# Giving a split tile's raw buffer to the next transfer as soon as its rest is told, in the v stage of a decoder trunk

## The chip, the cores and the metric

The kernel runs on one core of one Trainium2 chip. The metric is device microseconds of one execution, as a median over several runs. The core has TensorE (PE, with its weight loads shown apart as PEld), VectorE (DVE), ScalarE (ACT), GpSimd (POOL) and SyncE (SP). Work crosses between them by semaphores, and transfers from HBM are issued from the instruction streams of SP, ACT and POOL. Each of these streams is worked off in order: a transfer that has to wait for something holds up what stands behind it in the same stream.

## The reference, cut to what matters

Two pre-norm residual layers run over 256 positions with 1024 channels. The first mixes by attention and retention, the second by a gated short convolution; each is followed by a PEER mixer, which is where the change lies:

```python
def peer(xn, w_q, sub_keys, u, v):
    ...
    def step(args):
        tc, ec, gc = args
        hid = jax.nn.gelu(jnp.einsum('td,thkd->thk', tc, u[ec]), approximate=False)
        return jnp.einsum('thk,thkd->td', gc * hid, v[ec])
```

For each token 8 heads choose 16 of 16,384 experts. An expert has a row of u (1024 numbers) and a row of v (1024 numbers). The output is the sum of the chosen rows of v, weighted by gate times gelu of the token's product with the row of u. All of it is in f32.

## The kernel before

Of the 256 tokens, 96 are done sparsely: their 16,384-row tables are read by indirect transfers from POOL (L1020), 128 rows of 4 KB at a time, 96 such gathers from u and 96 from v in each layer. The other 160 tokens are done densely: the whole of u is multiplied with them, the hidden values are multiplied with a gate matrix that is zero where an expert was not chosen, and the result `HG` is multiplied with the whole of v. So a layer's PEER has a **u stage** and a **v stage** after the scores. The sparse gathers run beside both, one gather at a time being consumed by DVE (L1030 for u, L1041 for v, into `gacc`).

In the v stage v passes as 128 tiles of 128 experts by 1024 channels (512 KB each), in order, one tile a step. Most tiles are **split tiles** (the list `SPL`): ACT casts the raw tile to fp32r (`vhi`, `weight_parts`, L1419), DVE subtracts the cast from the raw tile and writes what is left as bf16 (`vlo`, `weight_rest`, L1426; below this is called telling the rest), and PE multiplies `vhi` with two parts of the hidden values (L1546) and `vlo` with a bf16 copy of them (L1548). After `vlo` is written nobody reads the raw tile again. Tiles 0, 2, 12, 22 and so on to 122, and the last three, are **whole tiles**: PE multiplies the raw tile itself (L1506). The hidden values of two or three neighbouring split tiles are split together by two casts on ACT (L1488, L1489) and one subtraction on DVE (`row_rest`, L1496).

What a step emits is written out by hand. At step i, `carry(i)` emits the `row_rest` of the group before, the casts of hidden values for a group that begins at tile i+3, the cast `vhi` of tile i+3, and the rest `vlo` of tile i+2. Then `st.next()` may issue loads and hands out tile i, PE's products of tile i are emitted, and `ga.step()` may let DVE consume one gather and POOL issue the next. `vhi` and `vlo` each rotate over three buffers.

The raw tiles lie in a ring of 8 buffers (`RAW`), filled by class `Stream`. Tile i uses buffer i mod 8, and loads are issued strictly in tile order (`self.nl` is the next one). In the v stage the loads of even tiles stand in SP's stream, those of odd tiles in ACT's (L151, `src[2]`). Whether the next load may be issued is decided when the program is written out, by `room()`, which asks `free()` of the tile that held the buffer before:

```python
        return i < 0 or (i < self.nu - self.held if self.whole(i) else i < self.ns)
```

A v tile is "whole" for this class (its entry in `srcs` has None), split or not, so it counts as free once it has been handed out and the next `st.next()` comes: at step i the newest load is that of tile i+7. This decides where in the stream the load stands. Beside it, the load carries semaphore waits for the instructions that really read the buffer before: `vlo` of the tile eight before it where that is a split tile, PE's products where it is whole.

Towards the end of the u stage (`i in (NK - QUIET, NK - QUIET + 2)`) `weight_parts` is called for v tiles 1 and 3 with their rests, so `weight_rest` also runs there.

Of the kernel before, what the change touches and what calls it, by code (L numbers as in the profile page):

```python
# [120 lines left out]
class Stream:  # L121
# [6 lines left out]
    def __init__(self, ctx, tc, srcs):  # L128
        self.nc = tc.nc
        self.srcs = srcs  # L130
        pool = ctx.enter_context(tc.tile_pool(name="wraw", bufs=1))
        self.ring = pool.tile([P, RAW, D], F32, tag="raw", name="raw")
        self.hi_pool = ctx.enter_context(tc.tile_pool(name="whi", bufs=3))
        self.lo_pool = ctx.enter_context(tc.tile_pool(name="wlo", bufs=3))
        self.more = None
        self.end = 0
        self.raw = {}
        self.part = {}
        self.nl = 0
        self.held = 0  # L140
        self.ns = 0
        self.nu = 0

# [43 lines left out]

    def free(self, i):

        return i < 0 or (i < self.nu - self.held if self.whole(i) else i < self.ns)  # L190

    def ahead(self, extra=0):
        n = len(self.srcs)
# [30 lines left out]
def trunk_kernel(ctx, tc, x, small, cst, mcst, ew_in, ew_out, ow_in, ow_out, wq, keys, pu, pe_, pv, pun, gains, out):  # L224
# [42 lines left out]
    st = Stream(ctx, tc, srcs)  # L267
# [12 lines left out]
    def nm(s):  # L280
        uid[0] += 1
        return f"{s}{uid[0]}"
# [770 lines left out]
    def peer(l, before, norm):  # L1053
        with tc.tile_pool(name=nm("hg"), bufs=1) as hp:
# [360 lines left out]
            def weight_parts(j, low=True):  # L1415

                raw = st.raw[first + j]
                whi[j] = st.hi_pool.tile([P, D], F32R, tag="hi", name=nm("vhi"))
                act.copy(whi[j], raw)  # L1419
                if low:  # L1420
                    weight_rest(j)

            def weight_rest(j):
                raw = st.raw[first + j]
                wlo[j] = st.lo_pool.tile([P, D], BF16, tag="lo", name=nm("vlo"))
                v.tensor_tensor(wlo[j], raw, whi[j].bitcast(F32), OP.subtract)  # L1426

            first = st.nu + NK - len(PRE)
            for i in range(NK):
# [82 lines left out]
            def carry(i):  # L1512
                j = i + AHEAD
                if "rest" in hsb:
                    row_rest()
                if 4 <= j and j in SPL:
                    if j in RUNS:
                        row_parts(j)
                    weight_parts(j, False)
                if 4 <= j - 1 and j - 1 in SPL:  # L1520
                    weight_rest(j - 1)
# [61 lines left out]
    with tc.manual_schedule():  # L1583
        norms = [Norm(0)]
        nc.sync.dma_start(G, small)
        nc.sync.dma_start(C[:, :P], cst[:, :P])
        for th in range(2):
            (nc.scalar if th else nc.sync).dma_start(h[:, th, :], x[th])
        nc.sync.dma_start(C[:, P:], cst[:, P:])
        v.memset(Z, 0.0)  # L1590
        act.activation(norms[0].w[:, 0, 6:7], Z[:, 0:1], AF.Sqrt)
        for _ in range(3):
            st._load()
        busy(24)
        norms[0].first(hid_tile(nm("junk")))
        a = Norm(1)
        even_mixer(norms[0], a)
        b = Folded(2)
        peer(0, a, b)
        a = Norm(3)  # L1600
        odd_mixer(b, a)
        peer(1, a, Final())
# [40 lines left out]
```

## Time and profile before

| what | value |
|---|---|
| median of 3 runs | 1489.08 us (1485.73 to 1489.53) |
| the profiled execution, as timed | 1486.53 us |
| its span, first to last instruction | 1484.7 us |
| granted TensorE clock, mean | 0.996 |
| HBM read | 527.93 MB |
| v stage of layer 0, products of tile 1 to the last tiles | about 494 us to 752 us |
| v stage of layer 1, the same | about 1215 us to 1475 us |

The span leaves out 1.8 us of the profiled execution's time. The clock is full nearly everywhere, so no stage is slow for that. The rows that matter are the chain that ended last, the wait table of the v stage, the tables of busy time and bandwidth by stretch, and the transfers' queues.

### The profile page before, as it was taken

The numbers are of one execution on the slowest core, as the hardware profiler recorded it, in microseconds if no ns is written. First come the engines' busy times: TensorE is split into PE (matmuls) and PEld (weight loads), VectorE is DVE, ScalarE is ACT, GpSimd is POOL, SyncE is SP. The second block draws the span as 40 slices with busy tenths as digits, with TensorE's granted clock in tenths as the row PEclk, the third lists the DMA queues.
The fourth block names the chain that finished last, engine by engine and source line by source line (L and its number), as shares of the span: only waits on it lengthen the run. The fifth ranks groups of instructions, "written<-read, shape, count | busy, mean of one in ns | idle before, by whom it ended". The sixth has DMA issues, their size and how long they took to land.

```text
span 1484.7 us, 30109 instructions
## 1 busy us (share of the span) xinstructions
PE 1434.1 (97%) x11260; PEld 1327.8 (89%) x11260; DVE 1242.5 (84%) x2505; ACT 804.1 (54%) x1872; POOL 731.1 (49%) x508
## 2 busy tenths in 40 slices
PE   9999999999998999899999999999999999999997
PEld 5667999999998999898898699999999999988887
DVE  5637999968898789999976589997888868999997
ACT  6556412158775555555663463213887745655554
POOL 6754545546664344443244374555655624653540
PEclk9999999999999999999999999999999999999999
DMA  8547899999999999999975589999999999999994
GB/s 323 198 146 253 324 369 393 397 413 412 411 412 407 385 398 405 402 407 408 384 264 180 179 307 346 388 402 404 411 413 410 402 392 396 389 407 406 405 408 172
DMA packets 132164, 531.81 MB, mean 358 GB/s; under 512 B 15217, under 2 KB 15473, under 8 KB 118705
## 3 DMA queue, kind: packets, MB, share of 16 engines
q1 hardware_dynamic: 57024, 257.95, 45.0%
q0 software_dynamic: 56416, 204.29, 34.8%
q10 hardware_dynamic: 18576, 67.64, 11.6%
q8 instruction: 89, 1.46, 0.4%
q14 instruction: 59, 0.48, 0.1%
HBM read 527.93 MB, written 1.05 MB: 356 GB/s over the span
## 4 chain that ended last, share of the span: by engine, by line
DMA 37%; PE 29%; DVE 24%; issue 5%; ACT 2%; POOL 1%; ACTq 0%; SPq 0%; DVEq 0%; POOLq 0%
DMA raw<-pv 25%; DMA rows<-pun,ig 7%; PE hid L1408 7%; DVE rows L1030 4%; PE vo L1546 4%; DMA grow<-pv,ig 3%; PE hid L291 2%; PE vo L1506 2%; DVE hg L1140 2%; DVE grow L1030 2%; DVE hg L1146 2%; DVE hg L1142 2%; PE vo L1548 2%; PE ea L325 2%; DMA rows<-pv,ig 2%
## 5 line engine op out<-in xcount | busy, mean ns | idle before, releaser
L1408 PE MATMUL hid<-xf,raw 128*128 128x160 f32 x3328 | 478.2, 301 | 8.8 <-DVE hg L1449 8.5
L1408 PEld LDWEIGHTS hid<-xf,raw 128*128 128x128 f32 x3328 | 458.2, 191 | 11.7 <-DVE hg L1449 11.6
L1419 ACT CAST vhi<-raw 128x1024 fp32r<-128x1024 f32 x222 | 227.4, 1047 | 205.7 <-DMA raw<-pv 143.1
L1546 PE MATMUL vo<-ko,vhi 128*128 128x320 f32 x1776 | 315.2, 319 | 14.8 <-DVE ko L1496 9.6
L1426 DVE TENSOR_TENSOR vlo<-raw,vhi 128x1024 bf16<-128x1024 f32 x222 | 268.0, 1223 | 47.6 <-ACT vhi L1419 43.2
L1020 POOL DMA_INDIRECT rows<-pv,ig x128 | 199.8, 1561 | 216.4 <-DVE gacc L1041 172.0
L1546 PEld LDWEIGHTS vo<-ko,vhi 128*128 128x128 f32 x1776 | 262.0, 188 | 21.3 <-ACT vhi L1419 14.2
L1020 POOL DMA_INDIRECT rows<-pun,ig x128 | 161.3, 1260 | 118.6 <-DVE rows L1030 61.6
L176 POOL TENSOR_TENSOR lo<-raw,hi 128x1024 bf16<-128x1024 f32 x70 | 167.2, 2397 | 87.0 <-ACT hi L174 80.3
L1030 DVE SCALAR_TENSOR_TENSOR rows<-rows,xg 128x1024 f32<-128x1024 f32 x128 | 155.4, 1220 | 23.6 <-DMA rows<-pun,ig 23.1
L1548 PE MATMUL vo<-hb,vlo 128*128 128x160 bf16 x1776 | 161.4, 234 | 7.1 <-DVE vlo L1426 6.8
L1446 ACT ACTIVATE hg<-hid 128x160 f32<-128x160 f32 (+14 forms) x240 | 62.2, 265 | 194.1 <-PE hid L1408 193.9
L1041 DVE SCALAR_TENSOR_TENSOR gacc<-rows,ghid,gacc 128x1024 f32<-128x1024 f32 x124 | 158.8, 1281 | 6.5 <-DMA rows<-pv,ig 6.2
L1020 POOL DMA_INDIRECT grow<-pv,ig x64 | 91.8, 1434 | 117.9 <-DVE gacc L1041 103.1
L1548 PEld LDWEIGHTS <-vlo 128*128 128x128 bf16 x1776 | 117.4, 98 | 34.1 <-DVE vlo L1426 14.3
L1358 ACT ACTIVATE ko<-ko,idxT 128x128 f16<-128x128 f16 x320 | 101.6, 391 | 38.2 <-DVE ko L1343 38.1
L1020 POOL DMA_INDIRECT grow<-pun,ig x64 | 82.8, 1293 | 78.9 <-DVE grow L1030 50.2
L174 ACT CAST hi<-raw 128x1024 fp32r<-128x1024 f32 x100 | 102.4, 1046 | 30.2 <-issue 19.9
L291 PE MATMUL hid<-x,hi 128*128 128x256 f32 x800 | 108.9, 289 | 3.9 <-DVE z L973 2.0
L291 PEld LDWEIGHTS hid<-x,hi 128*128 128x128 f32 x800 | 100.0, 193 | 4.8 <-issue 2.9
L1361 ACT ACTIVATE ko<-ko,idxT 128x128 f16<-128x128 f16 x320 | 101.2, 389 | 0.0
L1506 PE MATMUL vo<-hg,raw 128*128 128x160 f32 x544 | 83.1, 302 | 1.1 <-DVE hg L1449 1.1
(254 smaller groups left out, 2075.6 us busy)
## 6 DMA issues: line engine op xcount, KB each, us to landing
raw<-pu SPq DMA_DIRECT2D x104, 1024.0 KB, 8.3
raw<-pv SPq DMA_DIRECT2D x128, 512.0 KB, 8.5
raw<-pv ACTq DMA_DIRECT2D x128, 512.0 KB, 7.9
raw<-wq SPq DMA_DIRECT2D x32, 512.0 KB, 4.2
raw<-ew_in SPq DMA_DIRECT2D x28, 512.0 KB, 4.4
raw<-ow_in SPq DMA_DIRECT2D x24, 512.0 KB, 4.9
hg<-pe_ SPq DMA_DIRECT2D x22, 512.0 KB, 6.9
raw<-ew_out SPq DMA_DIRECT2D x8, 512.0 KB, 3.3
```

The source lines that it names most:

```text
L174: self.nc.scalar.copy(hi, t)
L176: eng.tensor_tensor(lo, t, hi.bitcast(F32), OP.subtract)
L291: pe.matmul(ps[:, :S], hi[:, k * P:(k + 1) * P], A2[:, k, s_, :], start=k == 0 and s_ == 0, stop=False)
L1020: gp.indirect_dma_start(self.row(s_), None, table, bass.IndirectOffsetOnAxis(IG[:, 0, s_ % STEPS:s_ % STEPS + 1].bitcast(U32), 0))
L1030: v.scalar_tensor_tensor(r, r, 1.0, XG[:, q % 2, :], op0=OP.mult, op1=OP.mult, accum_out=w)
L1041: v.scalar_tensor_tensor(self.acc[q], r, w, self.acc[q], op0=OP.mult, op1=OP.add)
L1408: pe.matmul(ps[:, :TD], w[k], XF[:, k, :], start=k == 0, stop=k == ND - 1)
L1419: act.copy(whi[j], raw)
L1426: v.tensor_tensor(wlo[j], raw, whi[j].bitcast(F32), OP.subtract)
L1506: pe.matmul(vo[b][:, TG:S], w[:, c], HG[:, i, :], stop=i == NK - 1, **m)
L1546: pe.matmul(vo[b][:, TG:S + TD], hi[:, b * P:(b + 1) * P], hs, **m)
L1548: pe.matmul(vo[b][:, TG:S], lo[:, b * P:(b + 1) * P], hb, **m)
```

## The change

`Stream` gets a set of dead tiles. `free()` says yes for a tile in it. `weight_rest` puts its tile there as soon as the subtraction that reads the raw tile last has been emitted, and asks at once for loads:

```diff
         self.held = 0
+        self.dead = set()
         self.ns = 0
...
     def free(self, i):
 
-        return i < 0 or (i < self.nu - self.held if self.whole(i) else i < self.ns)
+        return i < 0 or i in self.dead or (i < self.nu - self.held if self.whole(i) else i < self.ns)
...
                 v.tensor_tensor(wlo[j], raw, whi[j].bitcast(F32), OP.subtract)
+                st.dead.add(first + j)
+                st.loads()
```

`loads()` was there before; it issues loads as long as `room()` says yes. Loads still go in tile order, so a whole tile that has not been multiplied yet keeps back all that come after it.

## The prediction

> **What bounds the kernel now.** I read the page first: the slices of the span, then the chain that ended last.
>
> ```profile
> span 1484.7 us, 30109 instructions
> ...
> PE   9999999999998999899999999999999999999997
> ...
> GB/s 323 198 146 253 324 369 393 397 413 412 411 412 407 385 398 405 402 407 408 384 264 180 179 307 346 388 402 404 411 413 410 402 392 396 389 407 406 405 408 172
> ...
> DMA 37%; PE 29%; DVE 24%; issue 5%; ACT 2%; POOL 1%; ACTq 0%; SPq 0%; DVEq 0%; POOLq 0%
> DMA raw<-pv 25%; DMA rows<-pun,ig 7%; PE hid L1408 7%; DVE rows L1030 4%; PE vo L1546 4%; DMA grow<-pv,ig 3%; PE hid L291 2%; PE vo L1506 2%; DVE hg L1140 2%; DVE grow L1030 2%; DVE hg L1146 2%; DVE hg L1142 2%; PE vo L1548 2%; PE ea L325 2%; DMA rows<-pv,ig 2%
> ```
>
> PE is shown busy nearly all the time, yet the largest single piece of the chain, a quarter of the span, is the transfer of raw v tiles. A slice is 37.1 us, so the v stages are slices 14 to 20 and 33 to 40. The highest bandwidth in any slice is 413 GB/s. Next I read the two v stages by stretches: engines' busy time, granted clock, DMA share, GB/s.
>
> ```profile
> core 0: us, PE busy (x) PEld busy (x) DVE busy (x) ACT busy (x) POOL busy (x), PEclk, DMA share, GB/s
> 500.00:520.00 20.00, 20.00 (x178) 19.08 (x177) 18.88 (x19) 12.73 (x16) 12.43 (x7) 1.00 0.98 372
> 520.00:540.00 20.00, 20.00 (x178) 19.18 (x177) 17.01 (x16) 11.04 (x14) 9.37 (x6) 1.00 1.03 408
> 540.00:560.00 20.00, 20.00 (x178) 18.98 (x177) 18.72 (x18) 12.65 (x17) 7.25 (x5) 1.00 1.00 383
> 560.00:580.00 20.00, 20.00 (x178) 18.89 (x177) 18.23 (x19) 11.25 (x14) 9.89 (x6) 1.00 1.02 407
> 580.00:720.00 140.00, 131.47 (x1112) 120.80 (x1112) 130.71 (x123) 82.95 (x104) 59.17 (x39) 1.00 1.02 406
> ...
> 1210.00:1230.00 20.00, 19.78 (x166) 18.82 (x165) 15.46 (x18) 12.54 (x19) 3.90 (x3) 1.00 0.97 365
> 1230.00:1250.00 20.00, 20.00 (x177) 19.18 (x176) 18.44 (x19) 11.78 (x15) 9.50 (x6) 1.00 1.02 401
> 1250.00:1270.00 20.00, 20.00 (x179) 19.08 (x178) 16.91 (x17) 12.04 (x15) 7.56 (x5) 1.00 1.00 385
> 1270.00:1290.00 20.00, 20.00 (x178) 18.98 (x177) 19.96 (x20) 12.37 (x16) 15.44 (x7) 1.00 1.00 387
> 1290.00:1450.00 160.00, 150.06 (x1269) 137.63 (x1268) 148.52 (x139) 93.00 (x117) 76.03 (x45) 1.00 1.02 407
> ```
>
> A tile is 16 matmul records. There are two regimes. For the first 70 to 80 us PE sets the pace: 178 records in 20 us, or 20/(178/16) = 1.80 us a tile, while tiles loaded ahead are used up. After that it is 140/(1112/16) = 2.01 us a tile at 406 GB/s. What fills that stretch is shown by its transfers:
>
> ```profile
> DMA packets 15575, 56.84 MB, mean 406 GB/s; under 512 B 1731, under 2 KB 1731, under 8 KB 15561
> ...
> q0 software_dynamic: 5610, 20.42, 36.5%
> q1 hardware_dynamic: 5024, 18.30, 32.9%
> q10 hardware_dynamic: 4927, 17.94, 32.4%
> ...
> raw<-pv ACTq DMA_DIRECT2D x34, 512.0 KB, 7.9
> raw<-pv SPq DMA_DIRECT2D x34, 512.0 KB, 8.2
> rows<-pv,ig POOLq DMA_INDIRECT x27, 11.0
> grow<-pv,ig POOLq DMA_INDIRECT x12, 10.3
> ```
>
> 69.5 tiles and 39 gathers (POOL x39) of 0.524 MB make 56.9 MB, and 56.84 MB moved. The pace of the second regime is therefore (69.5 + 39) x 0.524 MB at 406 GB/s: bytes. The wait tables of 500 to 745 us (SP's own last) say who feels it:
>
> ```profile
> POOL rows L1020 <- DVE gacc L1041: 97.5, 39, 13.9
> ACT vhi L1419 <- DMA raw<-pv: 65.9, 37, 3.4
> ...
> DVE vlo L1426 <- ACT vhi L1419: 15.5, 23, 1.8
> ...
> SPq L151 <- DVE vlo L1426: 150.0, 44, 6.4
> ```
>
> The cast waits for raw tiles, 65.9 us in all; the rest waits for the cast, and PE behind both. The timeline of ACT and the chain show which raw tiles:
>
> ```profile
> 573.41 1.05 ACT L1419 CAST vhi<-raw 128x1024 fp32r<-128x1024 f32 x1 [1.85 <-DMA raw<-pv]
> 573.43 0.34 ACTq L151 DMA_DIRECT2D raw<-pv  x1
> 574.36 1.04 ACT L1419 CAST vhi<-raw 128x1024 fp32r<-128x1024 f32 x1
> ...
> 582.61 1.05 ACT L1419 CAST vhi<-raw 128x1024 fp32r<-128x1024 f32 x1 [0.86 <-DMA raw<-pv]
> ```
>
> ```profile
> 565.52 7.79 DMA raw<-pv
> 573.31 0.02 issue
> ```
>
> ACT casts an odd tile, issues the load of the odd tile four further on, and some 8 us later (7.79 from 565.52) its cast of that tile waits for this very load. That is a loop of one landing to four tiles. The even tiles, from SP, are cast 0.95 us after the odd one without a wait (574.36).
>
> **The change part by part.** It adds no work on any engine; it moves DMA issues within the streams of SP and ACT.
>
> Even tiles (SP's stream): nothing moves in time. SP issues only transfers, and what holds it is the wait for the rest of the buffer's tile (44 waits, 150.0 us). The buffer is already handed on the moment the rest is told. Half of the change is therefore void.
>
> Odd tiles (ACT's stream): before, the load of tile i+7 stands at step i, although the rest of tile i-1, whose buffer it takes, was emitted at step i-3. Now it stands at step i-3, behind the cast of that step. Loads go in tile order, so a whole tile holds them back: with tile 12 whole, load 20 waits for step 13, and then 20 to 23 are issued together. Of the odd loads 21, 23, 25, 27, 29, the first gains one step and the others three. A step is 1.80 to 2.01 us, so most odd loads leave up to 5.4 to 6.0 us earlier. At the start of v, load 9 moves from step 2 to 1, load 11 from 4 to 3, load 13 from 6 to 3.
>
> What that is worth differs by regime. In the second regime, the transfers of a tile (1.56 x 0.524 MB) take 2.01 us at 407 GB/s whenever they are issued. Both stretches run at 406 and 407, and no slice of the page exceeds 413. An earlier issue there only lengthens the landing. I take 0 and keep as ends 1.5% of the 300 us of both stretches (407 to 413), 4.4 us gained, and 0.
>
> In the first regime the transfers are not full. Against 407 GB/s the 20 us windows lack, in layer 0, (407-372) x 20 = 0.70 MB and (407-383) x 20 = 0.48 MB; in layer 1, 0.84, 0.12, 0.44 and 0.40 MB. PE needs more than the transfers can give there (0.82 MB in 1.80 us would be 455 GB/s), so every byte brought in early puts off the second regime. Odd buffers lying empty for three steps are what limits the transfers in flight, so I let the change fill these gaps. The first window of each layer I count by half: POOL waited up to 13.9 us for its first accumulation, so gathers were missing too, and loads 9 and 11 gain only a step. The sum is 0.35 + 0.48 + 0.42 + 0.12 + 0.44 + 0.40 = 2.21 MB, which at 407 GB/s is **5.4 us**. The ends are 0 and, with the first windows in full, 2.98 MB or 7.3 us.
>
> At the end of v the last loads also leave three steps sooner; the last steps' products are held by DVE's gathers, so I take 0 (ends 0 and 2 us a layer, about one tile).
>
> The price: ACT's load now waits for a rest that DVE has hardly begun, and ACT's stream stands until then. Behind it stand the casts of hidden values for the next group and the cast of tile i+4. The nearest rows are DVE's own:
>
> ```profile
> 505.82 1.28 DVE L1041 SCALAR_TENSOR_TENSOR gacc<-rows,ghid,gacc 128x1024 f32<-128x1024 f32 x1
> 507.02 0.65 DVE L1496 TENSOR_TENSOR ko<-hg,ko 128x480 fp32r<-128x480 f32 x1
> 507.58 2.36 DVE L1426 TENSOR_TENSOR vlo<-raw,vhi 128x1024 bf16<-128x1024 f32 x2
> ```
>
> The rest of an odd tile ends 1.05 + 1.2 = 2.3 us after its cast began, or up to 4.2 us if one accumulation (1.28) and one row rest (0.65) stand before it. ACT uses the first 2.1 us for the two casts. So it is held 0.2 to 2.1 us in every two steps of 3.6 to 4.0 us. It has the room: ACT is busy 82.95 of 140 us, so two steps leave it 1.6 us idle. And `vhi` rotates over three buffers, so a late cast has about two steps before PE needs it. I take 0. What it costs if that cover is gone is a rival below.
>
> At the end of u two calls put loads a little earlier behind the gelu, which already waits for the same product: 0.
>
> The sum against the profiled execution is 1486.53 - 5.4 = 1481.1 us. That execution lies 2.5 us below the median of the runs shown (1489.08), and the forecast for the median is 1489.08 - 5.4 = **1483.7 us**.
>
> **Rivals.** *Nothing to gain.* If the gaps of the first regime aren't due to the odd buffers but to PE's pace, or the whole tiles keep the ring in step, the loads only land later: 1487 to 1491, say 1489. For it: half the change is void, and 406 to 408 GB/s stand in four of the six late windows already. The Trainium skill speaks for it in "DMA: Bandwidth & Descriptors", section "Issuing engines are not separate DMA queues": transfers from all issuing engines interleave on the same 16 engines, so where they are issued saves only issue time. By that alone the sum would be 0. The trace agrees in the second regime (406 GB/s) and not in 500 to 520 us (372).
>
> *The gathers take the place of the raw tiles.* With more odd loads waiting, the three queues are backlogged together. Gathers carry 36.5% of the traffic in the full stretch; held to a third, one would land each 0.524/(406/3) = 3.87 us, or 39 in 151 us instead of 140. Raw tiles can run ahead only by about four more buffers, 2.1 MB or 5.2 us, so gathers come at most 5.2 us later, and then DVE waits for rows where it does not now. It cancels the gain, 1488 to 1492, say 1490. Against it: six row buffers let a gather take 6 x 140/39 = 21.5 us, and it lands in 11.0. The same page, section "Queues, rings and completion order", states such a turn-taking between queues, packet by packet; the trace's shares of 36.5, 32.9 and 32.4% do not show it either way.
>
> *ACT behind DVE: slower.* Held at the load, ACT makes the hidden values' casts and the next cast late, and DVE, whose stream is in order, waits for them at `row_rest` and the rest. DVE is busy 130.71 of 140 us, so it has (140-130.71)/34.75 = 0.27 us idle for each odd tile; the mechanism decides beyond that. At 0.5 us more waiting for each odd tile 0.23 us would reach the end, times the (1112+1269)/32 = 74 odd tiles of the second regimes, 17 us, less the gain of 5.4: 1501. It breaks even with the gain at 0.27 + 5.4/74 = 0.34 us.
>
> *The loop is the bound, not the bytes.* If landings of 8 us were latency and not queueing, seven tiles of lead instead of four would free the second regime down to DVE's 130.71/69.5 = 1.88 us a tile: 0.13 x 149 tiles = 19 us, so 1470. It would need 0.82 MB/1.88 us = 436 GB/s, above every slice.
>
> **How the numbers follow.** Chances: forecast (1480 to 1487) 0.50; nothing to gain 0.18; gathers 0.07; ACT behind DVE 0.15; loop 0.10. A measurement of this kernel can tell about 0.3%, 4.5 us, from no change. Of the forecast's half, seven in ten lie below 1484.6: 0.35 faster, 0.15 same. Nothing to gain gives 0.16 same and 0.02 slower, gathers 0.05 and 0.02, ACT behind DVE 0.15 slower, the loop 0.10 faster. Together 0.45, 0.36, 0.19. The range of 1474 to 1497 takes in the first three, the loop's nearer half, and ACT behind DVE up to a price of 13 us.
>
> **What would show it.** Right: in the changed profile the 20 us windows at the start of v stand near 407 GB/s, the cast's waits for raw tiles come later and are fewer, DVE waits for rows no more than now, and the stretches from 580 and 1290 us keep 2.01 us a tile. The odd landings are longer than 8 us. Wrong: those windows unchanged at 372 to 387 (nothing to gain); DVE `gacc` waiting for rows (gathers); `vlo` or `ko` rests waiting for ACT above 15.5 us in a layer (ACT behind DVE); or over 413 GB/s and below 1.95 us a tile (loop).

## The result, and the profile after

The kernel after takes 1480.18 us as a median of 14 runs, the kernel before 1487.34 us beside it. The ratio is 0.9947 with a 95% interval of 0.9934 to 0.996, so 5.9 to 9.8 us less. A second set of 12 runs, beside the experiments below, gave 0.9964 (0.9945 to 0.9983), 2.5 to 8.2 us less. The forecast of 5.4 us lies inside the second interval and just below the first; where the two overlap, the gain is 5.9 to 8.2 us. The profiled execution took 1480.22 us, its span is 1478.5 us.

Where the span went is told by the first and the last product of a cast tile in each v stage, here before, then after (the view of one line: count, duration, first and last start):

```profile
L1546 PE MATMUL vo<-ko,vhi x888: 302/309/418, 494.1 to 742.5; 128*128 128x320 f32 x178
...
L1546 PE MATMUL vo<-ko,vhi x888: 302/309/422, 1214.9 to 1465.1; 128*128 128x320 f32 x178
```

```profile
L1549 PE MATMUL vo<-ko,vhi x888: 302/309/472, 495.0 to 741.2; 128*128 128x320 f32 x178
...
L1549 PE MATMUL vo<-ko,vhi x888: 302/309/613, 1213.0 to 1458.4; 128*128 128x320 f32 x178
```

The first v stage shrank from 248.4 to 246.2 us, the second from 250.2 to 245.4: 7.0 us less, of which 0.8 was lost again outside; the span fell by 6.2. (Line numbers after are up to three higher.) The table of stretches after, same columns and windows as before:

```profile
500.00:520.00 20.00, 20.00 (x180) 18.98 (x179) 17.76 (x18) 13.15 (x16) 9.95 (x6) 1.00 1.00 390
520.00:540.00 20.00, 20.00 (x178) 19.18 (x178) 18.56 (x18) 11.24 (x14) 9.73 (x7) 1.00 1.03 409
540.00:560.00 20.00, 20.00 (x176) 19.08 (x175) 17.22 (x17) 10.70 (x13) 7.43 (x6) 1.00 1.00 397
560.00:580.00 20.00, 19.70 (x175) 18.50 (x174) 19.12 (x19) 13.58 (x19) 10.27 (x6) 1.00 1.03 407
580.00:720.00 140.00, 131.82 (x1125) 123.23 (x1125) 130.40 (x124) 84.26 (x105) 74.41 (x40) 0.99 1.03 408
...
1210.00:1230.00 20.00, 19.09 (x163) 18.03 (x162) 16.91 (x18) 12.96 (x18) 4.05 (x4) 1.00 0.93 344
1230.00:1250.00 20.00, 20.00 (x178) 19.18 (x177) 18.33 (x19) 12.19 (x15) 9.35 (x6) 1.00 1.03 409
1250.00:1270.00 20.00, 20.00 (x178) 19.08 (x177) 17.45 (x17) 11.98 (x15) 7.40 (x6) 1.00 1.02 400
1270.00:1290.00 20.00, 20.00 (x178) 18.98 (x177) 19.29 (x19) 12.32 (x16) 13.02 (x7) 1.00 1.03 408
1290.00:1450.00 160.00, 152.97 (x1303) 142.39 (x1301) 151.98 (x144) 96.58 (x121) 85.54 (x45) 0.99 1.03 408
```

The gaps of the PE-paced part are partly filled: 372 to 390, 383 to 397, 385 to 400, 387 to 408 GB/s. The first window of layer 1 is not (365 to 344; the stage begins 1.9 us earlier there, so the window is shifted by a tile). The byte-bound stretches stand at 408, where before they had 406 and 407. PE's pace in the first 80 us is unchanged, 175 to 180 records in 20 us in all but the first window of layer 1.

The starts of the split tiles' products (eight of the line above for each tile) tell in which part of the stage the time went. Both v stages added, one profiled execution each:

| from tile to tile | before | after | after, profiled again |
|---|---|---|---|
| 1 to 44 | 168.5 us | 168.4 us | 168.1 us |
| 44 to 83 | 161.6 us (2.07 a tile) | 153.2 us (1.96) | 154.9 us (1.99) |
| 83 to 124 | 166.3 us (2.03) | 167.8 us (2.05) | 167.6 us (2.04) |

The first third takes as long as before, the middle third gains 8.4 and 6.7 us, and the last third loses 1.5 and 1.3 us. The kernel holds PE's pace longer before the bytes set it.

The waits changed places. The wait table of 500 to 745 us, and the transfers of 580 to 720 us, after:

```profile
ACT ko L1491 <- DVE vlo L1427: 41.5, 20, 4.5
...
ACT vhi L1420 <- PE vo L1549: 32.4, 29, 2.8
ACT vhi L1420 <- DVE vlo L1427: 11.8, 7, 2.6
DVE vlo L1427 <- ACT vhi L1420: 9.1, 12, 2.1
DVE gacc L1042 <- DMA rows<-pv,ig: 7.2, 7, 2.0
...
ACT vhi L1420 <- DMA raw<-pv: 4.8, 5, 1.4
```

```profile
q0 software_dynamic: 5579, 20.31, 36.4%
q1 hardware_dynamic: 5035, 18.34, 32.9%
q10 hardware_dynamic: 5024, 18.31, 32.8%
...
raw<-pv ACTq DMA_DIRECT2D x34, 512.0 KB, 10.2
raw<-pv SPq DMA_DIRECT2D x34, 512.0 KB, 10.4
rows<-pv,ig POOLq DMA_INDIRECT x27, 19.0
```

The cast's wait for raw tiles is nearly gone (65.9 to 4.8 us). Raw landings are 2 us longer, gathered rows land in 19.0 instead of 11.0 us, and DVE now waits for them, 7.2 us. ACT has a new wait for the rest: 41.5 us ahead of the casts of hidden values and 11.8 us (before, 0.6) ahead of `vhi`, 53.3 us in 27 waits. One such place in ACT's timeline, and what the chain has at that time:

```profile
647.65 1.05 ACT L1420 CAST vhi<-raw 128x1024 fp32r<-128x1024 f32 x1 [0.73 <-PE vo L1549]
650.66 0.33 ACTq L152 DMA_DIRECT2D raw<-pv  x1
651.03 0.59 ACT L1491 CAST ko<-hg 128x480 fp32r<-128x480 f32 x1 [2.34 <-DVE vlo L1427]
```

```profile
649.41 1.22 DVE vlo L1427
650.63 1.20 DVE gacc L1042
...
652.09 20.98 DMA rows<-pv,ig
673.12 0.04 issue
673.17 1.30 DVE gacc L1042
...
674.73 19.92 DMA rows<-pv,ig
```

The rest ends at 650.63, the load leaves at 650.66, and the cast of hidden values behind it starts at 651.03 after ACT stood idle for 2.34 us. This is the hold that the prediction described. It had put it at 0.2 to 2.1 us; this one is just above that, the mean of the 27 is 2.0 us and the longest is 4.5 us. The chain here runs through gathers of 20 us, one round of the six row buffers.

### The profile page after: what moved, and what is told of

Same layout as the page of the kernel before. It is cut to its first block, busy times and chain, and to the rows that moved or that the text cites. A ratio compares the mean times of both kernels' runs of the same rounds, so it can differ in the third digit from the quotient of the medians.

```text
span 1478.5 us, 30169 instructions
## 1 busy us (share of the span) xinstructions
PE 1431.3 (97%) x11260; PEld 1329.0 (90%) x11260; DVE 1240.2 (84%) x2505; ACT 802.6 (54%) x1872; POOL 751.7 (51%) x508
## 4 chain that ended last, share of the span: by engine, by line
PE 37%; DVE 28%; DMA 23%; issue 7%; POOL 3%; ACT 2%; DVEq 0%; SPq 0%; ACTq 0%; POOLq 0%
PE vo L1549 9%; DMA rows<-pv,ig 7%; DMA grow<-pv,ig 6%; DMA rows<-pun,ig 6%; PE hid L1409 5%; PE vo L1551 5%; DVE rows L1031 4%; PE vo L1509 3%; PE hid L292 2%; DVE gacc L1042 2%; DVE vlo L1427 2%; DVE grow L1031 2%; DVE hg L1141 2%; DVE hg L1147 2%; DVE hg L1143 2%
## 5 line engine op out<-in xcount | busy, mean ns | idle before, releaser
L1021 POOL DMA_INDIRECT rows<-pv,ig x128 | 209.8, 1639 | 200.8 <-DVE gacc L1042 149.1
L1427 DVE TENSOR_TENSOR vlo<-raw,vhi 128x1024 bf16<-128x1024 f32 x222 | 265.9, 1218 | 30.3 <-ACT vhi L1420 26.7
L1021 POOL DMA_INDIRECT grow<-pv,ig x64 | 102.3, 1599 | 109.5 <-DVE gacc L1042 91.5
L1551 PEld LDWEIGHTS <-vlo 128*128 128x128 bf16 x1776 | 118.3, 98 | 32.8 <-DVE vlo L1427 11.6
L1491 ACT CAST ko<-hg 128x480 fp32r<-128x480 f32 (+1 forms) x76 | 44.0, 579 | 86.5 <-DVE vlo L1427 86.3
```

What stands on the lines that cost most here:

```text
L1021: gp.indirect_dma_start(self.row(s_), None, table, bass.IndirectOffsetOnAxis(IG[:, 0, s_ % STEPS:s_ % STEPS + 1].bitcast(U32), 0))
L1551: pe.matmul(vo[b][:, TG:S], lo[:, b * P:(b + 1) * P], hb, **m)
```

## The experiments

Ratios are to the kernel before, run beside each set, with their 95% intervals; microseconds are (1 - ratio) times some 1487.

**The first third alone, and the rest alone.**

```diff
+                if j < 44:
+                    st.dead.add(first + j)
+                    st.loads()
```

> The change for v tiles below 44 alone (the PE-paced first 80 us of each v stage); from tile 44 on as before. My theory (the gain is transfers that fill gaps in the PE-paced part, and the byte-bound part gains nothing by an earlier issue): nearly all of the gain, 5 to 7 us below before, ratio 0.995 to 0.997, with 2.0 us a tile after tile 44 and the cast waiting for raw tiles there again. Rival (the loop of one odd landing to four tiles was the bound of the second part): at most 2 us, ratio 0.999 to 1.0.

> The change for v tiles from 44 on alone (the byte-bound part and the end). My theory: 0 to 2 us below before, ratio 0.9985 to 1.0, although the cast's waits for raw tiles vanish there and DVE waits for gathered rows in their place. Rival (the loop of odd landings was the bound): all of the gain, 6 to 8 us, ratio 0.995 to 0.996.

 (The same with `if j >= 44`.)

The first third alone gave 0.998 (0.9965 to 0.9995), 3.0 us; the rest alone 0.9984 (0.9969 to 0.9998), 2.4 us. Neither point estimate is the whole gain, though the intervals are wide (0.7 to 5.2 and 0.3 to 4.6 us). Their sum, 5.4 us, agrees with the gain of the kernel after within the intervals. My theory of "nearly all in the first third" missed, and so did the rival's "all in the rest". The cast's wait for raw tiles in 580 to 720 us, in the first kernel, then in the second (48.7 us before):

```profile
ACT vhi L1420 <- DMA raw<-pv: 40.9, 24, 2.4
```

```profile
ACT vhi L1420 <- DMA raw<-pv: 19.1, 18, 2.5
```

Taking more than half of that wait away in the rest of v bought 2.4 us, not 30.

The second kernel also serves as a control for the windows of the first 80 us, since it changes next to nothing there. Its first windows stand at 360 and 311 GB/s against 372 and 365 before, so the first window of a layer differs too much from execution to execution to be read. The other six windows together moved 0.38 MB more than before without the change, 1.24 MB more in the first third alone, and 1.18 MB more in the kernel after. So the gaps are filled by the change, but about 0.4 MB of what the windows show can be chance.

By tiles, the first kernel takes 156.5 us from tile 44 to tile 83 and the second 154.3 us, against 161.6 before. From tile 1 to 44 they take 168.1 and 171.0 us. So each half of the change alone shortens the middle third, and the two do not simply add there.

**All loads in SP's stream.** On the kernel before, then on the kernel after:

```diff
-        r += [(pv[l, i], None, i % 2 == 1) for i in range(NK)]
+        r += [(pv[l, i], None, False) for i in range(NK)]
```

> The kernel before with all v loads in SP's stream, none in ACT's. SP issues on the data wait alone, so every raw buffer is handed on when its rest is told, without the change. My theory: as fast as after, or up to 2 us faster since ACT is not held at a load: ratio to before 0.993 to 0.996. Rival (SP holds odd loads behind even ones, whole tiles above all, or one queue for all raw tiles gets half of the turns instead of two thirds and raw tiles are late): no better than before, 0.998 to 1.003, with the cast waiting for raw tiles as before.

> The kernel after with all v loads in SP's stream. If the place in SP's stream is void, as I said of the even tiles, this is the same as the kernel before with all loads in SP's stream, within 0.1%. Rival: the earlier place matters on SP too (issue order, waits that count more than the data needs): 2 us or more apart.

The first gave 0.9966 (0.9951 to 0.9981), 5.1 us, just outside what I expected, the second 0.9979 (0.9965 to 0.9994), 3.1 us; their medians are 1482.55 and 1482.79 us. The two ratios are 0.13% apart, between my 0.1% and the rival's 2 us, and their intervals overlap; so no effect of the change on loads in SP's stream is seen, down to some 2 us. Moving the odd loads there gains about what the change gains. The waits of the first in 580 to 720 us show the rival's mark nevertheless:

```profile
ACT vhi L1419 <- DMA raw<-pv: 35.2, 39, 2.9
```

The cast still waits for raw tiles 35.2 us and DVE for no rows, the reverse of the kernel after, with the same time within the intervals. Which of the two streams of transfers is the late one made no difference that these runs resolve; that their sum sets the time is what this suggests. The Trainium skill, "DMA: Bandwidth & Descriptors", section "Queues, rings and completion order", says that a DMA engine takes turns between the queues that have work. The traces agree in direction: with raw tiles on two queues the gathers are late (19.0 us), with raw tiles on one queue they are not waited for.

**Less lead.** The buffer is given on one tile later, and two tiles later (`j - 1` in the second):

```diff
-                st.dead.add(first + j)
+                st.dead.update(first + n for n in SPL if n < j)
```

> The kernel after once more, as the reference for the runs beside it: 6 to 8 us below before.

> The raw buffer is given on one tile later (at the rest of the next tile): odd loads leave two steps earlier than before instead of three, and ACT no longer meets a rest that DVE has hardly begun. If the hold on ACT costs something, this is 1 to 3 us faster than after; if not, it lies between before and after, 4 to 6 us below before, since one step of lead is lost. My theory is the second.

> The raw buffer is given on two tiles later: odd loads leave one step earlier than before. If the gain grows with the lead, 2 to 3 us below before; if any lead over four tiles breaks the loop, all of the gain, 6 to 8 us.

0.9964 (0.9945 to 0.9983) with the full lead, 0.9967 (0.9948 to 0.9986) one tile later, 0.9975 (0.9956 to 0.9994) two tiles later. The order is that of a gain that grows with the lead, but the intervals don't separate the three. One tile later, ACT's waits for the rest fall from 53.3 to 8.5 us (500 to 745 us) and the cast again waits 26.0 us for raw tiles; the time is the same within the intervals. So no price of the hold is seen in the full kernel, but the intervals would hide one of 2 to 3 us.

**The hold ahead of the cast.**

```diff
+                if 4 <= j - 1 and j - 1 in SPL:
+                    weight_rest(j - 1)
                 if 4 <= j and j in SPL:
                     if j in RUNS:
                         row_parts(j)
                     weight_parts(j, False)
-                if 4 <= j - 1 and j - 1 in SPL:
-                    weight_rest(j - 1)
```

> After with carry's two parts swapped: the rest of tile i+2 and the load that waits for it now stand ahead of the casts of hidden values and of tile i+3 in ACT's stream, so that ACT's hold lies ahead of a cast that is due a step sooner; DVE's order is the same. My theory (the hold lies in ACT's idle time): within 2 us of after. Rival (ACT behind DVE has a price that is nearly reached): 5 us or more above after, with DVE's waits for the cast and the row casts above 20 us in a layer.

1.0316 (1.0284 to 1.0349): 47 us slower than before, and 51 us above the kernel after beside it (1534.84 and 1483.47 us). My theory fell here. The stretch of 580 to 720 us, and the waits of 500 to 720 us:

```profile
580.00:720.00 140.00, 122.11 (x1022) 111.33 (x1023) 119.51 (x112) 74.40 (x95) 47.57 (x36) 1.00 0.98 367
```

```profile
ACT ko L1491 <- DVE vlo L1427: 55.7, 20, 3.8
DVE vlo L1427 <- ACT vhi L1420: 30.8, 38, 1.5
...
ACT vhi L1420 <- DVE vlo L1427: 22.7, 9, 3.1
PEld vo L1549 <- ACT vhi L1420: 18.2, 21, 1.6
PE vo L1549 <- ACT vhi L1420: 13.6, 17, 1.4
```

ACT waits for DVE and DVE for ACT in turn, PE behind both: 140/(1022/16) = 2.19 us a tile, and the transfers drop to 367 GB/s. The pace is set by the hold, no longer by bytes. DVE's wait for the cast, 30.8 us, is the mark that the rival named.

**Fewer bytes.** Every second gather of v rows is left out, in the kernel before, the kernel after, and two variants:

```diff
+                if s_ >= STEPS and s_ % 2:
+                    continue
                 table = pun if s_ < STEPS else pv.rearrange("l i p d -> (l i p) d")
```

> The kernel before with every second gather of v rows left out (the products of those rows use what the buffer held; all of DVE's work stays). A tile then carries 1.28 instead of 1.56 transfers, 0.67 MB. My theory (bytes set the pace of the second part): landings shorten to 4 to 6 us, the second part falls from 2.01 to 1.83 to 1.90 us a tile, and the kernel is 15 to 25 us below before. Rival (an odd landing of 8 us is latency, and the loop of one landing to four tiles is the bound): landings stay near 8 us and the pace at 1.95 to 2.0, at most 5 us below before.

> The kernel after with the same gathers of v rows left out. My theory: with bytes to spare the earlier load has nothing to fill, so this is within 2 us of the kernel before with the same gathers left out. Rival (loop): 10 us or more below that one.

> The kernel after with all v loads in SP's stream and every second gather of v rows left out. If the 9.5 us by which the change made the kernel with fewer gathers slower are the hold on ACT's stream, they go here: 1442 to 1447 us, as the kernel before with fewer gathers (1445.5) or a little below it. If the earlier transfers themselves cost them (crowding, buffers, gathered rows that come later), it stays at 1452 to 1458.

> The buffer given on one tile later, loads of odd tiles in ACT's stream as after, and every second gather of v rows left out. If the hold is the cost, one tile later takes most of it away, since DVE has mostly told that rest by then: 1445 to 1450 us. If not, 1452 to 1458.

| loads of odd tiles, fewer gathers | median us | ratio |
|---|---|---|
| as before (ACT's stream, four tiles of lead) | 1445.52 | 0.9718 (0.9698 to 0.9737) |
| as after (ACT's stream, behind the rest) | 1455.03 | 0.9785 (0.9763 to 0.9807) |
| after, all in SP's stream | 1445.03 | 0.9715 (0.9699 to 0.9731) |
| given on one tile later, ACT's stream | 1447.36 | 0.972 (0.9699 to 0.9742) |

The second part of the first v stage with fewer gathers, as before and then as after:

```profile
580.00:720.00 140.00, 138.92 (x1218) 131.27 (x1216) 139.48 (x134) 91.66 (x113) 43.99 (x19) 1.00 0.98 359
```

```profile
580.00:720.00 140.00, 136.83 (x1190) 128.40 (x1188) 137.06 (x130) 88.39 (x111) 42.79 (x20) 1.00 0.96 350
```

```profile
ACT ko L1493 <- DVE vlo L1429: 40.2, 20, 2.9
...
ACT vhi L1422 <- DVE vlo L1429: 9.8, 7, 1.9
```

The kernel before, its loop of one odd landing to four tiles untouched, falls from 2.01 to 140/(1218/16) = 1.84 us a tile, inside the 1.83 to 1.90 expected: bytes were the bound, not a fixed landing time. The whole gain of 41 to 42 us is far more than the 15 to 25 us that I expected. The v stages, from the first to the last start of a cast tile's products, fell by 14 us each, and another 12 us lie outside them, where some of these gathers run too. PE and DVE are now both full (138.92 and 139.48 of 140 us). The landings that I expected at 4 to 6 us are not told by the profiles of the first two kernels; in the other two raw tiles land in 6.7 and 7.3 us, so nothing bears that part of the expectation out.

And here the change **costs** 9.5 us: 1.88 us a tile, with the same hold on ACT (the last two rows, 500 to 720 us) as in the full kernel. My expectation of "within 2 us" missed. The two last kernels say why: with the loads leaving as early but from SP's stream, or one tile later in ACT's (where ACT's waits for the rest are 2.6 instead of 40.2 us ahead of the casts of hidden values), the cost is gone. The two v stages together take 470.5, 480.4, 470.4 and 470.5 us in the four kernels, in the order of the table. It was the hold, not the earlier transfers.

## Why the prediction was right, and where its terms were not

- *Bytes bound the second regime.* Right. With half of the v gathers away the pace fell to 1.84 us a tile with the loop in place, and the two v stages lost 28 us. The kernel after takes the loop away, and from tile 83 on it still needs 2.05 us a tile. Both speak against the loop rival. No window of the tables shown went above 409 GB/s.
- *Even tiles: nothing.* Right as far as the runs resolve it: with all loads in SP's stream the two kernels differ by no more than their intervals. The trace of the kernel before shows why: of SP's 34 loads in 580 to 720 us, 26 leave 0.03 us after a rest has ended.
- *First regime, 5.4 us.* Right mechanism, about twice too large. The windows took in 18 + 1 + 14 + 0 and -21 + 8 + 15 + 21 GB/s over 20 us each, 1.12 MB or 2.8 us instead of 2.21 MB. For the six later windows the forecast was 1.44 MB and 1.18 came; the first two windows, counted with 0.77 MB, brought nothing that can be read. That part of the change alone gave 3.0 us (0.7 to 5.2). As forecast, the time was saved not in the first 80 us but by putting off the second regime: it lies between tiles 44 and 83. Not all of that can come from bytes brought in early, since the rest alone shortens the same tiles by 7.3 us in its profiled execution.
- *Second regime, 0.* Too small: the change from tile 44 on alone gave 2.4 us (0.3 to 4.6), within the end of 4.4 that I kept for it. 406 and 407 became 408 GB/s, 1.1 us over the 300 us; where the rest comes from, the end of the stage or the gathers that were put back, was not separated.
- *The total.* 5.4 us was forecast, and 7.2 us by the medians of the first set came. That it is so near is in part luck: one term was too large, the other too small, and neither is known to better than about 2 us.
- *The hold on ACT, 0.* No price is seen in the full kernel, but the reason given for it does not hold. I had counted ACT's idle time and two steps of slack, although my own upper end of 2.1 us was above the 1.6 us of idle time, and the holds measured 2.0 us on average. Where bytes do not set the pace the hold costs 9.5 us, and ahead of the casts of the step it costs 51 us. I take it that the full kernel pays nothing visible because its byte-bound pace of 2.0 us a tile is above the 1.88 that the hold allows; this is argued from the two paces, not shown by itself.
- *The gathers take the raw tiles' place.* It happened: DVE waits 7.2 us for rows, which I had named as the mark of this rival, landings are 19.0 us, and the chain runs through gathers. But it did not cancel the gain. The price I gave it, 5.2 us, was that of a delay. A delay of gathers can be paid for by raw tiles that came early, since both draw on the same 408 GB/s; the trace fits this, and no run tests it alone.
- *A reading.* For "nothing to gain" I wrote that 406 to 408 GB/s stood in four of the six late windows. Of the six windows of 20 us behind the first ones only two did (408 and 407); the other two figures are those of the long stretches. That made the rival look likelier than the lines did.

No kernel with the full work beats the kernel after beyond the intervals. The kernel before with all v loads in SP's stream comes to the same gain within them, with one expression changed and without the hold.

## What to carry to other kernels

Where transfers run at the highest rate that the profile shows (here 406 to 410 GB/s), ask of an earlier issue first what gaps in the bandwidth it can fill; a long wait for one transfer says who is late, not what it would bring to remove it. Look at the stream in which a load stands: here the data wait alone decided when most loads left SP's stream, which only issues transfers, and in the stream of ACT, which computes, each early load was also a wait of ACT. Such a hold can be hidden by another bound and come out when that bound goes, so try the change once with that bound lifted.

## What the runs showed of the hardware that was not expected

- What a load costs that waits at the head of ACT's stream depends on what else sets the pace, and on what stands behind it. In the full kernel 27 waits of ACT (53.3 us in one v stage) cost nothing that was seen, the 27 with fewer gathers (50.0 us in 500 to 720 us) cost 9.5 us, and with the load ahead of the casts of its step the price was 51 us. The Trainium skill, "DMA: Bandwidth & Descriptors", section "Issuing engines are not separate DMA queues", says that issuing from several engines saves only issue time. The full kernel agrees (1482.55 us from SP alone, 1483.47 us from both in a neighbouring set); with fewer gathers the measurement differs by 10 us, for the stream that is held.
- With three queues backlogged, gathers took the delay, from 11.0 to 19.0 us, and raw tiles from 8 to 10, at shares of 36.4, 32.9 and 32.8% that hardly moved.
